# RWKV stage of a four-layer hybrid step: reversed copy of the values in two halves, later root transposes, stores issued by ScalarE

## Chip, cores and metric

One core of a Trainium2 chip runs the whole program in one launch. The metric is the device time of an execution in microseconds; lower is better. Five engines appear in the profile: TensorE (PE, with its weight loads PEld), VectorE (DVE), ScalarE (ACT), GpSimd (POOL) and SyncE (SP), which only issues transfers. 16 DMA engines carry out what is issued.

## What is computed

One step of a backbone with four layers (retention, RWKV-7, differential attention, neighbourhood attention) over 640 tokens: 128 context tokens (a prompt) and 512 latent tokens, 1024 features, all float32. The change lies in the RWKV layer, whose core in the reference is:

```python
r, k, v, g = einsum('nbld,dne->nble', stack([x_r, x_k, x_v, x_g]), w_in)
kk = k * k_k;  kk = kk * rsqrt(max(sum(kk * kk, -1), 1e-12))      # 16 heads of 64
for dr in range(2):                                               # forward, backward
    decay = exp(-exp(-softplus(-(w0[dr] + tanh(x_w @ wA[dr]) @ wB[dr])) - 0.5))
    a = sigmoid(a0[dr] + (x_a @ aA[dr]) @ aB[dr])
    kd = k * (1 + (a - 1) * k_a)
    seq = (r, decay, kd, v, kk, a)
    if dr == 1: seq = flip(seq, time)
    y_d, s_d = scan(seq, s0[dr])    # s = s*w + (s @ -kk)(kk*a)^T + v k^T ;  y = s @ r
```

Each x_n is h + xx * mu[n], a mix of a token with its neighbours. The backward direction reads the values v in reversed order of time.

## The kernel before

The layer is done in two stages. `rwkv_project` makes k, r, v and g and writes each to DRAM, and prepares every pair of heads for the scan; `rwkv_mix` loads what was written and runs the chunked scan (chunks of 64 tokens) for the eight pairs of heads.

`rwkv_project` goes through the kinds k, r, v, g in this order. For each, `mix(n)` makes eight pieces of the mixed input (VectorE makes `wm`, ScalarE casts it to a high part `wxh`, VectorE takes the low part `wxl`), and a loop over four column panels `c2` loads 256 weight columns (`weights`, L160, on SP), splits them likewise into `wh` and `wl`, and multiplies in three passes (`mm3`, L88 to L90).

- For k and r the products go feature-major into PSUM tile `pj` (three buffers), ScalarE copies them to `wst` (L1166), and SP issues the store to `dr['k']`, `dr['r']` (L1174). For k ScalarE also squares them, and TensorE sums the squares per head into `nrm` (L1173).
- After k, VectorE takes the reciprocal roots `rn` of the 16 sums (`rsqrt`, tile `wny`, L124 to L129), TensorE transposes them in five pieces (L1189), ScalarE copies them out (L1190), and SP stores them to `dr['n']` (L1191). Then come two low-rank products (`low_rank(1)` with tanh for the decay, `low_rank(4)` for a), each with its own mix, under a higher priority.
- For v the products are token-major: five tiles of 128 tokens by 256 columns per panel, copied by ScalarE to `wvs` (two buffers, L1149), stored by SP (L1150). After the four panels SP issues two copies from DRAM to DRAM that make `vr`, in which the two halves of the columns change places (L1179): one for the 128 prompt rows, one for the 512 latent rows.
- For g ScalarE takes tanh (L1163), VectorE finishes `wst` (L1164), SP stores.

`rwkv_prepare` is a generator that prepares one pair of heads at a time; two pairs are started after each panel of r. For a pair it loads k, n (as kk) and r from DRAM (L1224 to L1227) and the second low-rank factors `wBr` (L1230), which ScalarE casts (L1232); then come decay, keys and queries, whose results go back to DRAM (bk L1268, q L1271, lt and lb L1286 and L1287), and the inverse of a triangular block (L1304 to L1316).

Each engine and SP run their queue strictly in order. The order on each queue is not written by hand: a planner places every instruction by its priority (the place in the code, raised inside `high_priority`) and by a simulated time of readiness. An instruction at the head of a queue that waits holds back all behind it. All 344,356 packets of the data queues belong to one queue, SP's; before the change no other engine issues a transfer.

Of the kernel before, what the change touches and what calls it, by code (L numbers as in the profile page):

```python
# [7 lines left out]
F32 = mybir.dt.float32  # L8
# [10 lines left out]
NP = 128  # L19
# [1053 lines left out]
class Rwkv:  # L1073
    def rwkv_project(s, hT, dr):

        nc, I = s.nc, s.I
        v, act, pe, gp = nc.vector, nc.scalar, nc.tensor, nc.gpsimd
        s.pj_bufs, s.wz_bufs = 3, 2
        with s.pool(name='w1', bufs=1) as w1, s.pool(name='w1p', bufs=1, space=PSUM) as pp:
            s.pp = pp  # L1080
            T = lambda shape, name, bufs=1, dt=F32: w1.tile(shape, dt, name=name, tag=name, bufs=bufs)
            xx = T([128, 8, NT], 'wxx')

            for k, shape in (('wN', [80, 32, 32]), ('wX', [80, 32, 32]), ('wBK', [128, NCH, 128]), ('wQ', [128, 2, NCH, 64]),
                             ('wLT', [128, NCH, 64]), ('wt1', [128, NT]), ('wt2', [128, NT]), ('wt4', [128, NT])):
                T(shape, k, s.pbufs.get(k, 1))
            for a, b in PARTS:
                for g in range(0, 8, s.xx_g):
                    e = gp if s.xx_p[g // s.xx_g] == 'p' else v
                    lo, hi = max(a - 1, 1), b - 1  # L1090
                    G = slice(g, g + s.xx_g)
                    edge = lambda t, src: e.tensor_copy(xx[:, G, t:t + 1], hT[:, G, src:src + 1])
                    e.tensor_tensor(out=xx[:, G, lo:hi], in0=hT[:, G, lo - 1:hi - 1], in1=hT[:, G, lo + 1:hi + 1], op=ALU.add)
                    if a == 0:
                        edge(0, 1)
                        edge(NP - 1, NP - 2)
                        edge(NP, NP + 1)
                    else:
                        edge(NT - 1, NT - 2)
                    lo, hi = (0, hi) if a == 0 else (lo, NT)  # L1100
                    v.scalar_tensor_tensor(out=xx[:, G, lo:hi], in0=xx[:, G, lo:hi], scalar=0.5, in1=hT[:, G, lo:hi], op0=ALU.mult, op1=ALU.subtract)

            def mix(n, cuts=(0, NT)):
                parts = [(T([128, NT], 'wxh', s.x_bufs, F32R), T([128, NT], 'wxl', s.x_bufs, F32R)) for _ in range(8)]
                for a, b in zip(cuts, cuts[1:]):
                    for kc in range(8):
                        m = T([128, NT], 'wm', 2)[:, :b - a]
                        v.scalar_tensor_tensor(out=m, in0=xx[:, kc, a:b], scalar=s.vc('rwkv_mu', 8 * n + kc), in1=hT[:, kc, a:b],
                                               op0=ALU.mult, op1=ALU.add)
                        s.split(*(p[:, a:b] for p in parts[kc]), m, v)  # L1110
                return lambda kc, sl: (parts[kc][0][:, sl], parts[kc][1][:, sl])

            def low_rank(n, W, parts_, fn):
                x_ = mix(n)
                w = s.weights_list([W[0], W[1]])
                for hf in range(2):
                    ps = s.proj_T(w, 0, hf, x_)
                    t = T([128, HV], 'wlr')
                    act.activation(out=t, in_=ps, func=fn)
                    s.split(parts_[0][:, hf * HV:hf * HV + HV], parts_[1][:, hf * HV:hf * HV + HV], t)  # L1120

            W = I['rwkv_w_in'][0]
            nrm = pp.tile([128, 2, 512], F32, name='wn', tag='wn')

            for k, n in (('pj', s.pj_bufs), ('pm', 1), ('wz', s.wz_bufs)):
                for _ in range(n):
                    pp.tile([128, 512], F32, name=k, tag=k, bufs=n)
            prep = None

            def step(kind, c2):  # L1130
                for _ in range(s.preps.get(kind, (0, 0, 0, 0))[c2]):
                    with s.tc.high_priority(s.hp[4]):
                        next(prep)

            for n, base, kind in ((2, 1024, 'k'), (0, 0, 'r'), (3, 2048, 'v'), (5, 3072, 'g')):
                if kind == 'g' and s.rate:
                    s.fill_rest()
                x_ = mix(n, (0, HV, NT) if kind == 'k' else (0, NT))
                if prep is None:
                    s.tw = [T([128, NT], f'wtw{j}', 1, F32R) for j in range(2)]  # L1140
                    s.ta = [T([128, NT], f'wta{j}', 1, F32R) for j in range(2)]
                    prep = s.rwkv_prepare(w1, pp, dr)
                    next(prep)
                for c2 in range(4):
                    w = s.weights(W[:, base + c2 * 256:base + c2 * 256 + 256])
                    if kind == 'v':
                        for tt in range(5):
                            st = T([128, 256], 'wvs', 2)
                            act.copy(st, s.proj_N(w, tt, 256, x_))  # L1149
                            nc.sync.dma_start(out=dr['v'][tt * 128:tt * 128 + 128, c2 * 256:c2 * 256 + 256], in_=st)  # L1150
                        step('v', c2)
                        continue
                    sts = [T([128, NT], 'wst', 2) for _ in range(2)]
                    if kind == 'k':
                        sqs = [T([128, NT], k) for k in ('wt1', 'wt2')]
                    for hf in range(2):
                        for cc in range(2):
                            c, st = c2 * 2 + cc, sts[cc]
                            ps = s.proj_T(w, cc, hf, x_)
                            sl = slice(hf * HV, hf * HV + HV)  # L1160
                            if kind == 'g':
                                th = T([128, HV], 'wth')
                                act.activation(out=th, in_=ps, func=AF.Tanh, scale=0.5)  # L1163
                                v.scalar_tensor_tensor(out=st[:, sl], in0=th, scalar=1.0, in1=ps, op0=ALU.add, op1=ALU.mult)  # L1164
                            else:
                                act.copy(st[:, sl], ps)  # L1166
                                if kind == 'k':
                                    act.activation(out=sqs[cc][:, sl], in_=ps, func=AF.Square, scale=s.vc('rwkv_kk', c))
                    for cc in range(2):
                        if kind == 'k':  # L1170
                            c = c2 * 2 + cc
                            for tt in range(5):
                                pe.matmul(nrm[:, 0, tt * 16:tt * 16 + 16], sqs[cc][:, tt * 128:tt * 128 + 128], s.ind[:, c, :], start=c + tt == 0, stop=c + tt == 11)  # L1173
                        nc.sync.dma_start(out=dr[kind][c2 * 2 + cc], in_=sts[cc])  # L1174
                    if kind in 'rg':
                        step(kind, c2)
                if kind == 'v':
                    for a, b in ((0, NP), (NP, NT)):
                        nc.sync.dma_start(out=dr['vr'][a:b].rearrange("t (a w) -> a t w", a=2),  # L1179
                                          in_=dr['v'][a:b].rearrange("t (a w) -> a t w", a=2)[:, ::-1])  # L1180
                if kind == 'k':
                    n2, y_, t_ = (T([128, 80], k) for k in ('wn2', 'wny', 'wnt'))
                    v.tensor_scalar(out=n2, in0=nrm[:, 0, :80], scalar1=1e-12, scalar2=None, op0=ALU.max)
                    rn = s.rsqrt(w1, n2, None, None, y_, t_)
                    rt = T([128, NT], 'wst', 2)[:16]
                    for a, b in ((0, 4), (4, 5)):
                        ps = pp.tile([128, 512], F32, name='pj', tag='pj', bufs=s.pj_bufs)
                        for tt in range(a, b):
                            pe.transpose(ps[:16, (tt - a) * 128:(tt - a) * 128 + 128], rn[:, tt * 16:tt * 16 + 16], s.ident)  # L1189
                        act.copy(rt[:, a * 128:b * 128], ps[:16, :(b - a) * 128])  # L1190
                    nc.sync.dma_start(out=dr['n'], in_=rt)  # L1191
                    with s.tc.high_priority():
                        low_rank(1, I['rwkv_wA'][0], s.tw, AF.Tanh)
                        low_rank(4, I['rwkv_aA'][0], s.ta, AF.Copy)

    def rwkv_prepare(s, pool, pp, dr):
# [649 lines left out]
```

## Time and profile before

| | us |
|---|---|
| median of 3 runs | 2610.86 |
| lowest and highest | 2610.16, 2616.23 |
| profiled execution | 2608.0 |
| its span, first to last instruction | 2606.2 |

The page gives TensorE 89% of the span, VectorE 58%, ScalarE 41%, GpSimd 26%. The span in 40 slices is 65.2 us a slice; the RWKV projection lies between about 750 and 1185 us (slices 12 to 18), the scan after it up to about 1585 us. In the views by stage each engine's time is busy time in the window, followed by its count of instructions; PEclk is the share of full TensorE clock that was granted; DMA is the mean busy share of 16 DMA engines. In a timeline a row gives the start, the duration and, in brackets, how long the engine stood idle before it and for whom.

### The profile page before, as it was taken

To read this page: it belongs to the slowest core of one execution; us is meant where nothing else is said; L and a number is where in the kernel's file an instruction comes from. 1 tells how busy PE (TensorE), PEld (TensorE's weight loads), DVE (VectorE), ACT (ScalarE), POOL (GpSimd) and SP (SyncE) were. 2 spreads that over 40 slices of the span, in tenths; PEclk is the share of its full clock that TensorE was granted. 3 is DMA by queue.
4 is the path that set the end of the run, shared out by engine and by line. 5 is a ranking of instruction groups with operands and counts; after the bars stand their busy time and mean duration, and the time that the engine had idled before them with its cause. 6 is when DMAs were issued, how large, how long until landed. Compare 5 with 4: busy or idle time off the path is not lost.

```text
span 2606.2 us, 48698 instructions
## 1 busy us (share of the span) xinstructions
PE 2308.8 (89%) x18951; PEld 2086.3 (80%) x18951; DVE 1500.5 (58%) x3511; ACT 1067.3 (41%) x2405; POOL 675.5 (26%) x576
## 2 busy tenths in 40 slices
PE   7999999997988999294888997889889888999998
PEld 5888888987958889194777877688888887898888
DVE  7534343443173898394888554657776665645554
ACT  5323233332153655152333342245554433645551
POOL 3323232303210000001243433233222323332321
PEclk9999999998988889695888888899999998999999
DMA  8433333225272566367365645511111122223321
GB/s 294 131 101 102 118 101 110 90 85 188 83 262 69 166 191 216 107 193 182 102 148 136 160 126 177 175 56 48 45 55 39 51 68 56 67 76 78 77 71 57
DMA packets 344586, 303.54 MB, mean 116 GB/s; under 512 B 140220, under 2 KB 281044, under 8 KB 344356
## 3 DMA queue, kind: packets, MB, share of 16 engines
q1 hardware_dynamic: 344356, 300.44, 38.8%
q8 instruction: 149, 2.44, 0.4%
q14 instruction: 81, 0.66, 0.1%
HBM read 231.37 MB, written 64.79 MB: 114 GB/s over the span
## 4 chain that ended last, share of the span: by engine, by line
PE 34%; DVE 14%; DMA 4%; issue 3%; ACT 3%; SPq 3%; POOL 1%; ACTq 0%; DVEq 0%; POOLq 0%
PE pj L88 5%; PE pj L89 5%; PE pj L90 5%; PE oa L88 2%; PE oa L89 2%; PE oa L90 2%; DVE wtmp L1310 2%; DVE wX L1312 1%; PE nO L1024 1%; PE wsc L1439 1%; PE dtp L839 1%; PE wch L1507 1%; PE npt L1007 1%; PE wy L1541 1%; SPq L160 1%
## 5 line engine op out<-in xcount | busy, mean ns | idle before, releaser
L93 POOL TENSOR_TENSOR wl<-wr,wh 128x1024 fp32r<-128x1024 f32 (+1 forms) x168 | 371.2, 2222 | 628.5 <-ACT wh L170 490.4
L88 PE MATMUL pj<-hH,wh 128*128 128x320 f32 x1280 | 408.2, 321 | 10.5 <-ACT hH L96 7.1
L89 PE MATMUL pj<-hL,wh 128*128 128x320 f32 x1280 | 406.7, 318 | 3.0 <-POOL hL L93 2.4
L90 PE MATMUL pj<-hH,wl 128*128 128x320 f32 x1280 | 404.1, 316 | 0.1
L88 PEld LDWEIGHTS pj<-hH,wh 128*128 128x128 f32 x1280 | 246.4, 193 | 24.3 <-ACT hH L96 10.4
L89 PEld LDWEIGHTS pj<-hL,wh 128*128 128x128 f32 x1280 | 247.1, 193 | 10.6 <-POOL hL L93 3.8
L90 PEld LDWEIGHTS pj<-hH,wl 128*128 128x128 f32 x1280 | 246.5, 193 | 2.4 <-issue 1.0
L170 ACT CAST wh<-wr 128x1024 fp32r<-128x1024 f32 x168 | 175.5, 1047 | 133.7 <-PE pj L89 48.6
L88 PE MATMUL oa<-oh,wh 128*128 128x384 f32 (+1 forms) x640 | 201.6, 316 | 20.6 <-ACT wh L170 14.4
L89 PE MATMUL oa<-ol,wh 128*128 128x256 f32 (+1 forms) x640 | 199.3, 313 | 0.1
L88 PE MATMUL pj<-wh,hH 128*128 128x256 f32 x640 | 188.4, 294 | 12.2 <-DVE dr L756 7.4
L90 PE MATMUL oa<-oh,wl 128*128 128x256 f32 (+1 forms) x640 | 199.1, 312 | 0.0
L89 PE MATMUL pj<-wl,hH 128*128 128x256 f32 x640 | 186.0, 291 | 0.0
L90 PE MATMUL pj<-wh,hL 128*128 128x256 f32 x640 | 185.4, 290 | 0.0
L88 PE MATMUL pj<-wxh,wh 128*128 128x320 f32 x416 | 132.8, 327 | 53.2 <-DVE wst L1164 44.8
L88 PEld LDWEIGHTS pj<-wh,hH 128*128 128x128 f32 x640 | 127.5, 199 | 20.3 <-DVE dr L756 8.3
L88 PEld LDWEIGHTS oa<-oh,wh 128*128 128x128 f32 x640 | 122.8, 192 | 23.7 <-ACT wh L170 16.3
L89 PE MATMUL pj<-wxl,wh 128*128 128x320 f32 x416 | 134.5, 325 | 2.2 <-DVE wxl L93 2.2
L90 PE MATMUL pj<-wxh,wl 128*128 128x320 f32 x416 | 133.8, 323 | 1.9 <-DVE wl L93 1.9
L88 PEld LDWEIGHTS pj<-wxh,wh 128*128 128x128 f32 x416 | 82.1, 199 | 58.1 <-DVE wst L1164 45.1
L89 PEld LDWEIGHTS pj<-wl,hH 128*128 128x128 f32 x640 | 127.7, 200 | 0.0
L90 PEld LDWEIGHTS pj<-wh,hL 128*128 128x128 f32 x640 | 127.5, 199 | 0.0
(479 smaller groups left out, 5601.0 us busy)
## 6 DMA issues: line engine op xcount, KB each, us to landing
wr<-in_ret_w_in SPq DMA_DIRECT2D x48, 512.0 KB
wm<-in_w_mod SPq DMA_DIRECT2D x40, 512.0 KB
wr<-in_w_mod SPq DMA_DIRECT2D x32, 512.0 KB
wr<-in_rwkv_w_in SPq DMA_DIRECT2D x32, 512.0 KB
wl<-in_w_mod SPq DMA_DIRECT2D x24, 512.0 KB
wr<-in_diff_w_in SPq DMA_DIRECT2D x48, 256.0 KB
wr<-in_na_w_in SPq DMA_DIRECT2D x48, 256.0 KB
wd_bk<-wBK SPq DMA_DIRECT2D x16, 640.0 KB
```

The source lines that it names most:

```text
L88: mm(out, l[0], r[0], start=start, stop=False)
L89: mm(out, l[0], r[1], start=False, stop=False)
L90: mm(out, l[1], r[0], start=False, stop=stop)
L93: eng.tensor_tensor(out=lo, in0=src, in1=hi.bitcast(F32), op=ALU.subtract)
L160: nc.sync.dma_start(out=raw[:, :, c:c + x.shape[1]], in_=x[j * 128:(j + 4) * 128].rearrange("(k p) c -> p k c", p=128))
L170: nc.scalar.copy(hi[:, :, :n], raw[:, :, :n])
L839: pe.matmul(po, at[:, j * 128:j * 128 + 128], v_[:, vt, cc * 128:cc * 128 + 128], start=j == 0, stop=j == nt - 1)
L1007: pe.transpose(pt[:, j * 128:j * 128 + 128], P[:, j * 128:j * 128 + 128], s.ident)
L1024: pe.matmul(ot_ps[i * 64:i * 64 + 64, oc:oc + 128], vt[j][:, hc:hc + 64], pts[i][:, j * 128:j * 128 + 128], start=j == 0, stop=j == len(vt ...
L1310: v.tensor_tensor(out=t, in0=X_[:, 0:j + 1, j:j + 1].to_broadcast([80, j + 1, n]), in1=N_[:, j:j + 1, j + 1:].to_broadcast([80, j + 1, n]) ...
L1312: v.tensor_tensor(out=X_[:, 0:j + 1, j + 1:], in0=X_[:, 0:j + 1, j + 1:], in1=t, op=ALU.subtract)
L1439: pe.matmul(ps[:, u - u0, :], QT[:, u, :], TT[:, u, :], start=True, stop=True)
```

## The change

In the v loop, after panels 1 and 3, the reversed copy is issued for the 512 columns that are then complete, split in eight blocks of 64 columns instead of two of 512; the copy after the loop goes. The layout that readers of `vr` see is made by the reversed order of the blocks. The stores of k, r, v and n are issued by ScalarE; those of g stay on SP. The transposes of the roots, their copies and their store stand after the first low-rank product and inside its higher priority.

```diff
                             act.copy(st, s.proj_N(w, tt, 256, x_))
-                            nc.sync.dma_start(out=dr['v'][tt * 128:tt * 128 + 128, c2 * 256:c2 * 256 + 256], in_=st)
+                            act.dma_start(out=dr['v'][tt * 128:tt * 128 + 128, c2 * 256:c2 * 256 + 256], in_=st)
+                        if c2 % 2:
+
+                            hc = slice(c2 // 2 * 512, c2 // 2 * 512 + 512)
+                            for a, b in ((0, NP), (NP, NT)):
+                                blocks = [dr[k][a:b, hc].rearrange("t (a w) -> a t w", a=8) for k in ('vr', 'v')]
+                                nc.sync.dma_start(out=blocks[0], in_=blocks[1][:, ::-1])
                         step('v', c2)
                         continue
...
-                        nc.sync.dma_start(out=dr[kind][c2 * 2 + cc], in_=sts[cc])
+                        (nc.sync if kind == 'g' else act).dma_start(out=dr[kind][c2 * 2 + cc], in_=sts[cc])
                     if kind in 'rg':
                         step(kind, c2)
-                if kind == 'v':
-                    for a, b in ((0, NP), (NP, NT)):
-                        nc.sync.dma_start(out=dr['vr'][a:b].rearrange("t (a w) -> a t w", a=2),
-                                          in_=dr['v'][a:b].rearrange("t (a w) -> a t w", a=2)[:, ::-1])
                 if kind == 'k':
...
                     rn = s.rsqrt(w1, n2, None, None, y_, t_)
-                    rt = T([128, NT], 'wst', 2)[:16]
-                    for a, b in ((0, 4), (4, 5)):
-                        ps = pp.tile([128, 512], F32, name='pj', tag='pj', bufs=s.pj_bufs)
-                        for tt in range(a, b):
-                            pe.transpose(ps[:16, (tt - a) * 128:(tt - a) * 128 + 128], rn[:, tt * 16:tt * 16 + 16], s.ident)
-                        act.copy(rt[:, a * 128:b * 128], ps[:16, :(b - a) * 128])
-                    nc.sync.dma_start(out=dr['n'], in_=rt)
                     with s.tc.high_priority():
                         low_rank(1, I['rwkv_wA'][0], s.tw, AF.Tanh)
+                        rt = T([128, NT], 'wst', 2)[:16]
+                        for a, b in ((0, 4), (4, 5)):
+                            ps = pp.tile([128, 512], F32, name='pj', tag='pj', bufs=s.pj_bufs)
+                            for tt in range(a, b):
+                                pe.transpose(ps[:16, (tt - a) * 128:(tt - a) * 128 + 128], rn[:, tt * 16:tt * 16 + 16], s.ident)
+                            act.copy(rt[:, a * 128:b * 128], ps[:16, :(b - a) * 128])
+                        act.dma_start(out=dr['n'], in_=rt)
                         low_rank(4, I['rwkv_aA'][0], s.ta, AF.Copy)
```

## Rows read from the trace of the kernel before

**Rows 1.** The page: busy time of the engines; busy tenths in 40 slices (TensorE).
```profile
PE 2308.8 (89%) x18951; PEld 2086.3 (80%) x18951; DVE 1500.5 (58%) x3511; ACT 1067.3 (41%) x2405; POOL 675.5 (26%) x576
...
PE   7999999997988999294888997889889888999998
```
**Rows 2.** Busy time by stage; columns: window, length, five engines, PEclk, DMA share, GB/s.
```profile
824.60:836.10 11.50, 0.00 (x0) 0.00 (x0) 11.38 (x25) 3.25 (x5) 0.00 (x0) 0.51 0.30 82
...
850.00:880.00 30.00, 25.90 (x156) 23.10 (x156) 29.32 (x40) 20.33 (x40) 0.00 (x0) 0.77 0.26 87
880.00:940.00 60.00, 60.00 (x503) 58.10 (x500) 47.92 (x82) 33.92 (x80) 0.00 (x0) 1.00 0.74 230
...
960.00:1034.00 74.00, 71.51 (x665) 68.62 (x665) 65.00 (x123) 41.22 (x97) 1.12 (x2) 0.94 0.70 215
...
1061.40:1085.00 23.60, 0.00 (x0) 0.00 (x0) 0.00 (x0) 0.00 (x0) 0.00 (x0) 0.55 0.13 51
1085.00:1098.70 13.70, 0.00 (x0) 0.00 (x0) 0.00 (x0) 0.00 (x0) 0.00 (x0) 0.50 0.54 162
...
1106.20:1111.80 5.60, 5.60 (x22) 5.32 (x22) 5.56 (x16) 1.98 (x4) 3.52 (x1) 0.51 0.90 244
1111.80:1180.00 68.20, 62.07 (x531) 58.53 (x532) 62.06 (x140) 35.12 (x80) 4.18 (x8) 0.97 0.61 185
```
**Rows 3.** SP's issues in order of time: start, duration, line, tensors, count.
```profile
1033.71 0.69 SPq L1179 DMA_DIRECT2D wd_vr<-wd_v  x1
1034.50 5.69 SPq L1286 DMA_DIRECT2D wd_lt<-wLT  x2
...
1051.04 0.61 SPq L1179 DMA_DIRECT2D wd_vr<-wd_v  x1
1051.75 33.14 SPq L160 DMA_DIRECT2D wr<-in_rwkv_w_in  x1
1084.99 4.62 SPq L1271 DMA_DIRECT2D wd_q<-wQ  x1
1089.70 1.19 SPq L1230 DMA_DIRECT2D wBr<-in_rwkv_aB  x1
```
**Rows 4.** Waits, 740 to 1120 us: total us, times, longest us.
```profile
PE pj L88 <- DVE wst L1164: 44.8, 1, 44.8
PE pj L1189 <- DVE wny L129: 11.6, 1, 11.6
PE pj L88 <- ACT wvs L1149: 6.3, 1, 6.3
...
ACT wB L1232 <- DMA wBr<-in_rwkv_aB: 47.1, 5, 40.4
ACT wvs L1149 <- DMA wd_v<-wvs: 20.9, 7, 8.0
```
**Rows 5.** DMA view, 1060 to 1075 us: packets, MB, share of 16 engines.
```profile
q1 hardware_dynamic: 374, 0.77, 13.1%
```
**Rows 6.** DMA view, 1212 to 1216 us, and SP's timeline just before.
```profile
q1 hardware_dynamic: 2732, 0.66, 76.3%
...
1208.70 5.67 SPq L1415 DMA_DIRECT2D wR<-wd_q  x4
```
**Rows 7.** DMA view, 1176 to 1180 us, mostly stores of lt and lb.
```profile
q1 hardware_dynamic: 1970, 0.28, 47.0%
```
**Rows 8.** The chain that ended last: two loads of wBr, start and duration.
```profile
1014.00 2.31 DMA wBr<-in_rwkv_aB
...
1089.70 9.03 DMA wBr<-in_rwkv_aB
```
**Rows 9.** VectorE's timeline around the roots.
```profile
832.54 0.82 DVE L93 TENSOR_TENSOR wxl<-wm,wxh 128x640 fp32r<-128x640 f32 x1
...
844.06 0.89 DVE L1235 SCALAR_TENSOR_TENSOR wkk<-wkk,wkkh,wk__8958 128x640 f32<-128x640 f32 x1 [7.97 <-DMA wkk<-wd_n]
```
**Rows 10.** Line L1150: SP's issues of the v stores, ns min, median, max.
```profile
L1150 SPq DMA_DIRECT2D wd_v<-wvs x20: 319/339/1358, 967.3 to 1049.1; - x20
```

## The prediction

> **What bounds the kernel now.** I read four views in this order: busy share by slice, busy time by stage, the SP queue in order of time, and who waited for whom. TensorE is busy 89% of the span, so it is the engine to watch. But the slice row has a hole: slice 17 of 40 (1042 to 1107 us) shows a 2 where its neighbours show 9 [rows 1]. The stage table puts numbers on it: from 1061.4 to 1098.7 us, 37.3 us, TensorE, VectorE, ScalarE and GpSimd all do nothing, while the 16 DMA engines are only 0.13 busy at 51 GB/s for the first 23.6 us of it [rows 2]. A stretch in which no engine computes can only be waiting for a transfer, and whatever shortens it moves all later work forward one for one.
>
> The SP queue tells which transfer. At 1051.04 SP issues the second part of the reversed copy vr<-v (512 rows, 2048 KB, L1179). The next issue, a weight load, takes 33.14 us where a v store takes 0.34 [rows 10]; the one after it 4.62 us; only at 1089.70 comes wBr, a 64 KB load [rows 3]. ScalarE stood 40.4 us for that wBr, VectorE and TensorE stood behind ScalarE, TensorE for 44.8 us [rows 4]. So a small load that the decay step needs was queued on SP behind a big copy. Its 0.13 busy share is 2/16: the copy has two column blocks as its outer count and runs on two engines. In 15 us inside the hole 374 packets of 2 KB took 13.1% of 16 engines: 15 x 16 x 0.131 / 374 = 84 ns each [rows 5]. 1024 such rows on two engines are 512 x 84 ns = 43 us, which is the hole. The first part of the copy (128 rows, issued 1033.71) does the same on a small scale: 128 x 84 ns = 10.8 us, in which SP needs 5.69 us for two small issues, and TensorE stands 6.3 us for a ScalarE copy whose buffer waits for a v store queued there [rows 3, 4].
>
> **The change, part by part.** All against the profiled execution (2608.0 us, span 2606.2); the median of the runs shown, 2610.9, is 2.9 above it.
>
> *1. The last copy.* The new copy of 512 columns moves 64-column pieces (256 B), outer count 8. From outer count 2 on two engines I take 8 on eight engines. The second half's large part is then 512 x 8 = 4096 pieces, 512 per engine: the count per engine is as before, so all depends on what a 256 B piece costs. Nearest row: a stretch with only such loads (242 B a packet) gives 4 x 16 x 0.763 / 2732 = 17.9 ns. Stores of 128 B to DRAM, mixed with some loads, give 4 x 16 x 0.47 / 1970 = 15.3 ns. The upper bound is what SP itself needed for four loads of 640 such pieces: 5.67 us for 160 per engine, 35 ns [rows 6, 7]. So 9.2 to 18 us instead of 43. SP was held 38 us (1051.75 to 1089.7), 0.9 of the 43; now 8 to 16. wBr is issued 22 to 30 us earlier and lands in 2.3 us as at 1014 [rows 8], or again in 9.0 (1089.70 to 1098.73). Gain 22 to 37; I take 30, near the load row.
>
> In a sentence by itself: the Trainium skill (DMA: Bandwidth & Descriptors, Why a DMA increments its semaphore by 16 and not by 1) says that a transfer uses the largest number of engines up to 16 that divides the outermost counts of both sides, which would make it 8 for the new copy; the trace's 2/16 for outer count 2 agrees, and no run here yet shows the 8.
>
> *2. The small part of the last copy.* 128 pieces per engine at 17.9 to 35 ns, 2.3 to 4.5 us, instead of 10.8. The 6.3 us stand mostly goes: gain 3 to 6.3, I take 5. The v store in it also leaves SP's queue.
>
> *3. The new copies in the middle.* After panel 1 of v, SP gets 128 + 512 pieces per engine: 11.5 us (to 22) in a stretch where it used to hold nothing up. Queued behind them on SP are the weight panels of v, the bk, q and lt stores, and the k, kk, r and wBr loads, for which ScalarE and VectorE wait in order. The row nearest in length is the small part above: an 11 us hold cost TensorE 6.3 us. Loss 0 to 13; I take 5, since two v panels are by then often loaded.
>
> *4. The roots.* Today TensorE stands 11.6 us at the transposes of L1189 for the last of the reciprocal roots, which VectorE makes between the pieces of mix(1) [rows 4]. Later, TensorE does the first low-rank product there. But that product needs all eight pieces of mix(1), the last at 833.4 [rows 9] against 836.1 for the roots, and VectorE was 11.4 of 11.5 us busy in the gap [rows 2]. TensorE thus gets ahead by its first product, some 9 us. Against it: the n store comes after the product instead of before, and VectorE stood 8.0 us for kk, which is loaded from n [rows 9]; it would stand some 3 to 4 us longer, and from 850 to 880 it is the bound (29.3 of 30 us) [rows 2]. Between a gain of 12 and a loss of 4 I take a gain of 4.
>
> *5. The clock.* After the hole TensorE runs at 0.51 of its clock, the 1.2 GHz level, for the 5.6 us from 1106.2 [rows 2]; at full clock that is 2.8. Gain 0 to 4, taken as 2, as the smaller holes may still cost some.
>
> *6. Stores issued by ScalarE.* 8 + 8 + 20 + 1 = 37 issues. No row shows one on ScalarE; on SP the v stores take 0.32 to 1.36 us, median 0.34 [rows 10]. That is 12.6 us of ScalarE time, in stages where it is busy 33.9 of 60 and 41.2 of 74 us [rows 2], so most lies in its idle time; three PSUM buffers cover a 0.34 us later eviction. On the good side ScalarE stood 20.9 us for v stores to land [rows 4], 8.0 of them already in term 2; but TensorE lost only 74 - 71.5 = 2.5 us from 960 to 1034 [rows 2], so no more can come back. SP no longer waits for the k and r copies either; but the weights queued behind those stores were in time (TensorE busy 60.0 of 60 us from 880 to 940 [rows 2]), so that is worth nothing. From a gain of 2.5 to a loss of 12.6; I take a loss of 1.
>
> Sum: -30 - 5 + 5 - 4 - 2 + 1 = -35 us. 2608.0 - 35 = 2573, and some 2 more for the median: 2575 us.
>
> **Rivals.**
>
> *The pieces cost the same whatever their size* (the slower case). At 84 ns for 256 B too, each half's large part holds SP 38 us, and there are two: two holes of 45 in place of 45 + 6.3, +39, less 4 for the roots: about 2645. The hole grew from 6.3 to 45 as SP's hold went from 11 to 38 us; on that line two holds cost as much as today at 25 us each, that is from about 53 ns a piece. For it: nobody has copied DRAM to DRAM in 256 B pieces in this trace. Against it: 17.9 and 15.3 ns for loads and stores of this size [rows 6, 7]. In a sentence by itself: the Trainium skill (DMA: Bandwidth & Descriptors, Specifications) asks for at least 512 B for line rate and says that below it a read-modify-write is done, which speaks against this cut; the rows agree as far as 256 / 17.9 = 14 B/ns against 2048 / 84 = 24 go. Chance 6%.
>
> *ScalarE is held too.* If its issues wait while SP's big copy is being fed, ScalarE stands 8 to 16 us in the middle of v, with v stores of panel 2 in its queue, and TensorE behind it. Some 12 us more than term 3: 2587. For: every issue on SP was held then; against: the hold is seen on one queue alone [rows 3]. Chance 12%.
>
> *VectorE is the bound behind the hole.* It is busy 65 of 74 us before and 62 of 68 us from 1111.8 on [rows 2]; if it sets the pace, terms 2, 4 and 5 vanish (they are TensorE's), and the middle hold is its too: 30 - 8 - 1 = 21, 2590. Chance 14%.
>
> *Everything covered.* The middle copy costs nothing, the last is at its 9 us end, the roots give 8: 37 + 6 + 8 + 4 = 55, 2556. Chance 12%.
>
> *The order is not as written.* The order on every queue is worked out by a planner, so the copies and transposes can stand elsewhere than in the code; then almost any part of terms 1 and 3 may go, with the time around 2605. Chance 4%.
>
> **How the numbers follow.** The forecast, 2562 to 2588, has 52%. The range 2552 to 2600 takes in the forecast, the held ScalarE, the VectorE bound and most of the all-covered case; outside are the slower case, the order and the tails. A difference of 0.3% (7.8 us) is about what can be told from none: faster, below 2603, 0.88; same 0.05; slower 0.07.
>
> **What would show it.** Right: no stretch above 1000 us in which all engines are idle for over 15 us; during the copies DMA share near 0.5 instead of 0.13 and about 110 GB/s; the longest SP issue behind a copy 6 to 16 us; TensorE's stand at L1164 under 20 us; L1189 no longer in its waits; stores of k, r, v on a ScalarE queue at 0.3 to 0.4 us. Wrong: issues of 30 us after both large copies (the slower case), a ScalarE issue of over 5 us (held), VectorE above 95% with TensorE idle from 1000 on (VectorE bound).

## The result, and the profile after

| | us |
|---|---|
| before, in the same session | 2610.98 |
| after, median of 4 runs | 2586.49 (2578.95 to 2591.24) |
| ratio, with its 95% interval | 0.9899 (0.9868 to 0.9931) |
| profiled execution of after, its span | 2591.24, 2589.2 |
| after, measured again beside the experiments | 2581.52, ratio 0.9884 (0.9855 to 0.9913) |

By the two ratios the change gains 26 and 30 us. Line numbers of after are higher by up to 6 (v stores still L1150, copies L1156, g L1170, transposes L1193, KK load L1414).

One thing told ahead of the prediction was wrong: in the copy it is the time axis `t` that `[:, ::-1]` reverses, in both kernels. The blocks `a` only cut the columns, so any number of them gives the same `vr`; their number decides nothing but how the transfer is cut.

The page's busy tenths of TensorE: the 2 in slice 17 of [rows 1] is gone; slices 17 to 19 have 8, 6 and 5.
```profile
PE   7999999997989898865898987899899898999998
```
SP's issues of after in order of time (columns as in [rows 3]): the first half's big copy, the second half's, and what stands behind each.
```profile
998.06 0.69 SPq L1156 DMA_DIRECT2D wd_vr<-wd_v  x1
998.84 11.17 SPq L1288 DMA_DIRECT2D wd_lt<-wLT  x2
...
1011.58 0.46 SPq L1306 DMA_DIRECT2D wN<-wd_lt  x1
...
1045.92 0.67 SPq L1156 DMA_DIRECT2D wd_vr<-wd_v  x1
1047.69 8.54 SPq L1273 DMA_DIRECT2D wd_q<-wQ  x1
...
1056.85 1.02 SPq L1232 DMA_DIRECT2D wBr<-in_rwkv_aB  x1
```
The hold behind the last copy fell from 33.14 us [rows 3] to 8.54, and wBr is issued 11 us after the copy instead of 39. The waits of after, 740 to 1240 us, answer [rows 4]:
```profile
PE wtp L1424 <- DMA wKK<-wd_q: 34.1, 1, 34.1
PE wz L88 <- ACT wt L1246: 11.2, 7, 6.9
PE pj L1193 <- DVE wny L129: 4.3, 1, 4.3
...
ACT wB L1234 <- DMA wBr<-in_rwkv_aB: 8.9, 4, 4.0
ACT wE L1253 <- DMA wd_lb<-wLT: 8.4, 1, 8.4
ACT wvs L1149 <- DMA wd_v<-wvs: 6.7, 4, 4.0
```
The stand of 44.8 us is gone, ScalarE's for wBr went from 47.1 to 8.9. But TensorE's wait for KK, the first load of the scan, grew to 34.1 us. In before it was, in the same view from 1180 to 1240 us:
```profile
PE wtp L1422 <- DMA wKK<-wd_q: 18.0, 1, 18.0
```
By stage (columns as in [rows 2]):
```profile
960.00:1034.00 74.00, 65.33 (x603) 63.05 (x600) 55.08 (x101) 39.20 (x89) 1.10 (x2) 0.93 0.70 205
1043.00:1066.40 23.40, 15.27 (x117) 13.63 (x116) 20.62 (x32) 13.00 (x31) 3.30 (x3) 0.84 0.70 186
1066.40:1142.00 75.60, 68.81 (x560) 65.16 (x560) 65.89 (x149) 37.55 (x83) 5.44 (x9) 0.94 0.65 196
1142.00:1198.00 56.00, 13.04 (x280) 10.86 (x280) 25.48 (x81) 8.81 (x16) 5.61 (x5) 0.52 0.77 185
```
The last row is the new bottleneck: 56 us between the last g and the first product of the scan, with TensorE busy for 13. In before this way takes 35.9 us, with TensorE busy for 13.6. Within it all engines but SP stand still from 1169.8 to 1186.8 us, 17 us in which only transfers run; in before it is 12.

**Stretches.** Two profiles of one instruction order can stand some 8 us apart before anything that was changed (kernel before: 825.4 us at the clamp of the sums of which the roots are taken; the experiment before_eight: 833.1). So I read stretches between landmarks, from the first and last start of a line: v copies (L1149), g (L1164, now L1170), first product of the scan (L1439, now L1441), first product of the next layer (L117). Before, then after; columns: duration in ns as least, median, greatest, then first and last start:
```profile
L1149 ACT COPY wvs<-pj x20: 350/372/378, 963.6 to 1048.7; 128x256 f32<-128x256 f32 x20
L1164 DVE SCALAR_TENSOR_TENSOR wst<-wth,pj x16: 455/476/486, 1105.7 to 1180.1; 128x320 f32<-128x320 f32 x16
L1439 PE MATMUL wsc<-wTT,wQT x320: 274/275/582, 1216.0 to 1532.9; 128*128 128x128 f32 x160
```
```profile
L1149 ACT COPY wvs<-pj x20: 353/372/383, 959.3 to 1043.0; 128x256 f32<-128x256 f32 x20
L1170 DVE SCALAR_TENSOR_TENSOR wst<-wth,pj x16: 469/478/489, 1066.4 to 1142.1; 128x320 f32<-128x320 f32 x16
L1441 PE MATMUL wsc<-wTT,wQT x320: 275/275/583, 1198.4 to 1508.4; 128*128 128x128 f32 x160
```
The same landmarks, read in every profile, in us; "to scan" is the sum of the five columns before it, "all" goes from the clamp of the sums to the next layer, the last column is (1 - ratio) x 2611 from the timed runs:

| kernel | clamp to v | v | v to g | g | g to scan | to scan | all | gained |
|---|---|---|---|---|---|---|---|---|
| before | 138.2 | 85.1 | 57.0 | 74.4 | 35.9 | 390.6 | 889.6 | |
| after | 128.2 | 83.7 | 23.4 | 75.7 | 56.3 | 367.3 | 865.0 | 26 |
| after_again | 128.9 | 84.6 | 22.1 | 74.0 | 57.9 | 367.5 | 861.9 | 30 |
| before_eight | 137.9 | 78.4 | 28.1 | 73.7 | 35.9 | 354.0 | 855.6 | 31 |
| only_copy | 138.1 | 77.9 | 20.5 | 71.0 | 41.1 | 348.6 | 849.0 | 45 |
| only_stores | 134.6 | 69.5 | 62.3 | 72.0 | 51.7 | 390.1 | 889.3 | 2 |
| only_roots | 130.3 | 88.1 | 10.8 | 102.5 | 58.6 | 390.3 | 882.6 | 7 |
| copy_stores | 134.6 | 73.2 | 21.4 | 68.1 | 51.4 | 348.7 | 845.5 | 55 |
| copy_roots | 130.5 | 80.7 | 22.8 | 73.5 | 41.6 | 349.1 | 849.3 | 39 |
| inverse_first | 128.1 | 80.6 | 20.4 | 70.6 | 58.0 | 357.7 | 843.2 | 50 |
| after_redrawn | 127.9 | 85.4 | 23.9 | 74.7 | 47.7 | 359.6 | 847.0 | 40 |
| pool_copy | 127.2 | 86.9 | 12.3 | 66.5 | 65.2 | 358.1 | 847.4 | 34 |
| no_copy | 128.7 | 72.1 | 16.1 | 66.8 | 70.1 | 353.8 | 845.6 | 46 |
| after_sixteen | 128.2 | 84.0 | 21.3 | 75.8 | 57.7 | 367.0 | 860.1 | 33 |

So up to the last g the change gains 10.0 + 1.4 + 33.6 - 1.3 = 43.7 us, and 20.4 are lost again between the last g and the scan.

Two cautions. A stretch holds waiting and work, and the work differs, since the planner lays other preparation into it (689 products of TensorE in v of after, 641 in that of copy_stores). And the stages that no edit touches differ too: the scan up to the next layer takes 485 to 502 us in these profiles, the rest of the kernel 882 to 893. So "to scan" is the cleanest column for what an edit did in its own stages, and "gained" for what came of it.

### The profile page after: what moved, and what is told of

The parts are those of the page before. It is cut to its first block, busy times and chain, and to the rows that moved or that the text cites. A ratio compares the mean times of both kernels' runs of the same rounds, so it can differ in the third digit from the quotient of the medians.

```text
span 2589.2 us, 48673 instructions
## 1 busy us (share of the span) xinstructions
PE 2319.3 (90%) x18951; PEld 2090.2 (81%) x18951; DVE 1501.1 (58%) x3511; ACT 1070.2 (41%) x2405; POOL 670.7 (26%) x576
## 5 line engine op out<-in xcount | busy, mean ns | idle before, releaser
L88 PE MATMUL pj<-hH,wh 128*128 128x320 f32 x1280 | 407.9, 321 | 11.4 <-ACT hH L96 7.8
L89 PEld LDWEIGHTS pj<-hL,wh 128*128 128x128 f32 x1280 | 246.7, 193 | 11.4 <-DVE hL L93 3.8
L88 PE MATMUL pj<-wh,hH 128*128 128x256 f32 x640 | 190.0, 297 | 11.4 <-DVE dr L756 6.7
L89 PEld LDWEIGHTS oa<-ol,wh 128*128 128x128 f32 x640 | 123.1, 193 | 1.1 <-DVE ol L93 0.9
```

Source lines behind the costliest of these rows:

```text
L88: mm(out, l[0], r[0], start=start, stop=False)
L89: mm(out, l[0], r[1], start=False, stop=False)
```

## Experiments: the parts alone

`only_copy` is the kernel before with the copy in halves of eight blocks, `only_stores` with the stores on ScalarE, `only_roots` with the transposes later; `no_copy` is after with the copies taken out: the backward direction then reads v itself, and the reversal in time is left out. The edit of no_copy:

```diff
-                            for a, b in ((0, NP), (NP, NT)):
-                                blocks = [dr[k][a:b, hc].rearrange("t (a w) -> a t w", a=8) for k in ('vr', 'v')]
-                                nc.sync.dma_start(out=blocks[0], in_=blocks[1][:, ::-1])
...
-                        src = dr['vr' if d else 'v'][:, cols]...
+                        src = dr['v'][:, cols]...
```

> Only the reversed copy in halves of eight blocks; stores stay on SP, the transposes stay where they were. If the hole behind the big copy is what the change removes, this gives nearly all of it: no stretch of 37 us with all engines idle, SP's longest issue behind a copy 8 to 12 us, about 2586 to 2592 us against 2611. If the stores on ScalarE are what frees SP (rival), it gives less than half: above 2600.

Measured: 2563.24 us, ratio 0.9826 (0.981 to 0.9841). The copy alone gains 45 us, more than the whole change and some 23 more than expected; the longest group of issues behind a copy on SP took 8.00 us, and between 700 and 1300 us no stretch with all engines idle is longer than 11.3 us.

> Only the stores of k, r, v and n issued by ScalarE. If the big copy is the cause, its 33 us issue and TensorE's stand of some 45 us stay, and the time stays within 4 us of 2611. If SP's waits for the k, r and v copies were what held it, the time falls by 10 us or more.

Measured: 2607.65, ratio 0.9993 (0.9974 to 1.0011): nothing that can be told. The stage with the v panels becomes 15.6 us shorter (69.5), since the v stores no longer wait behind SP's holds, but the hole behind the copy stays, now before another instruction, and takes it back ("to scan": 390.1, before 390.6):
```profile
PE wn L1280 <- ACT wLT L1281: 45.6, 6, 33.7
```

> Only the transposes of the roots after the first low-rank product. My term was a gain of 4 us (bounds: gain of 12, loss of 4): about 2607. If VectorE is the bound there, TensorE's 11.6 us are given back before the r stage ends: 2611, or up to 4 us slower since n is stored later.

Measured: 2604.61, ratio 0.9972 (0.9954 to 0.9989). 7.9 us are gained ahead of v, but the hole is still there, inside g, and by the scan's start none of them is left (390.3); what the timed runs show, 7 us, lies in the scan:
```profile
PE pj L88 <- DVE wst L1164: 36.7, 2, 36.1
```

> The changed kernel without any reversed copy: the backward direction reads v itself, so the reversal in time of the values is left out. What the copies still cost: if the hold of SP in the middle (11 us on SP, 6.9 us of TensorE) and at the end (8.5 us on SP, 5.7 us of TensorE) reach the end of the kernel, about 13 us less than the changed kernel, 2573, and more (to 2565) if the late load for the second inverse goes too. If what follows the projection absorbs them, 2586 as the changed kernel.

Measured: 2563.65, ratio 0.9824 (0.9807 to 0.984). Compared with after, the new copies still cost 16 to 20 us in that kernel; but only_copy, which has them, is as fast. So the parts gain 45, 2 and 7 us alone and 26 to 30 together: some 25 us are lost where they meet.

## Experiments: the block count

`before_eight` is the kernel before with one number changed, and every instruction stands where it stood; `after_sixteen` likewise is after.

```diff
-                        nc.sync.dma_start(out=dr['vr'][a:b].rearrange("t (a w) -> a t w", a=2),
-                                          in_=dr['v'][a:b].rearrange("t (a w) -> a t w", a=2)[:, ::-1])
+                        nc.sync.dma_start(out=dr['vr'][a:b].rearrange("t (a w) -> a t w", a=8),
+                                          in_=dr['v'][a:b].rearrange("t (a w) -> a t w", a=8)[:, ::-1])
```

> The kernel before, with its whole copy in one piece and in its place, but eight blocks of 128 columns for two of 512; every instruction stands where it stood. It tells what the block count does alone. As the prediction has it (the copy's time goes by the number of blocks that stand outermost): SP's hold behind the big copy falls from 33.1 to 12 to 20 us, the hole on TensorE from 44.8 to 24 to 32, and the time to 2588 to 2597. If the halves alone had done it (less to copy behind the last panel): 2604 to 2612. If a piece costs the same whatever its size (four times the pieces): the hold passes 100 us, the time 2670.

Measured: 2580.74, ratio 0.988 (0.9854 to 0.9906), a gain of 31 us, 7 beyond the forecast for it. SP behind the whole copy of 2048 KB, then the waits:
```profile
1051.67 0.67 SPq L1179 DMA_DIRECT2D wd_vr<-wd_v  x1
1052.44 11.41 SPq L160 DMA_DIRECT2D wr<-in_rwkv_w_in  x1
1063.94 0.89 SPq L1271 DMA_DIRECT2D wd_q<-wQ  x1
1064.92 0.42 SPq L1230 DMA_DIRECT2D wBr<-in_rwkv_aB  x1
```
```profile
PE pj L88 <- DVE wst L1164: 15.2, 1, 15.2
```
The hold went from 33.14 to 11.41 us and the hole from 44.8 to 15.2, both below what was expected, with nothing else changed. The block count alone does what the whole change does. The halves add the 14 us between this kernel and only_copy, together with the other order that the planner made for them.

> The whole change with sixteen blocks of 32 columns in each half for eight of 64; every instruction stands where it stood. If the copies' time goes by the number of blocks up to 16: SP's holds behind the big copies fall from 11 and 8.5 to 4 to 6 us, and the time by 4 to 12 us, to 2574 to 2583. If at eight blocks the number of pieces already sets the pace (the trace shows some 1.8 ns from one 256-byte piece to the next): twice the pieces make the holds 15 to 20 us, and the time 2592 to 2605.

Measured: 2578.61, ratio 0.9875 (0.9845 to 0.9905), against 0.9884 (0.9855 to 0.9913) beside it: no difference. The holds fell by 2.5 and 0.5 us, from 10.30 and 7.52 in after_again, less than either theory had them change:
```profile
1000.72 7.85 SPq L1288 DMA_DIRECT2D wd_lt<-wLT  x2
...
1047.01 7.05 SPq L1273 DMA_DIRECT2D wd_q<-wQ  x1
```
The DMA view of 1050 to 1056 us, during a big copy, of after (eight blocks) and then of after_sixteen; packets, MB, share of 16 engines. Beside them the two blocks of before have [rows 5].
```profile
q1 hardware_dynamic: 3085, 0.79, 57.7%
```
```profile
q1 hardware_dynamic: 5838, 1.20, 135.3%
```
Two blocks are 0.131 x 16 = 2.1 engines' worth of packets, eight are 9.2, and sixteen more than all 16, so packets lie over one another in the records there. A record of a 256-byte piece is 6 x 16 x 0.577 / 3085 = 18.0 ns long, the loads' value in the prediction. The Trainium skill's rule of the outermost counts (DMA: Bandwidth & Descriptors, Why a DMA increments its semaphore by 16 and not by 1) has 2, 8 and 16 engines: the trace agrees, with 2.1, 9.2 and more than 16, as far as overlapping records can tell; that it was eight engines and not nine is not shown.

## Experiments: where the parts meet

`copy_stores` and `copy_roots` leave one part out. `inverse_first` and `after_redrawn` are after with another priority for some transfers (the copies; the loads of N), and `pool_copy` is after with the copies on GpSimd's queue; the edits of these three, in this order:

```diff
+                                with s.tc.high_priority(-3000 if c2 == 1 else 1):
-                                nc.sync.dma_start(out=blocks[0], in_=blocks[1][:, ::-1])
+                                    nc.sync.dma_start(out=blocks[0], in_=blocks[1][:, ::-1])
...
+        with s.tc.high_priority(20000):
-        nc.sync.dma_start(out=N_, in_=dr['lt'][p].rearrange("b i u s t -> (b i u) s t"))
+            nc.sync.dma_start(out=N_, in_=dr['lt'][p].rearrange("b i u s t -> (b i u) s t"))
...
-                                nc.sync.dma_start(out=blocks[0], in_=blocks[1][:, ::-1])
+                                gp.dma_start(out=blocks[0], in_=blocks[1][:, ::-1])
```

> The copy in halves and the stores on ScalarE, the roots' transposes where they were. The parts alone gave -46 (copy), -2 (stores) and -5 us (roots), the whole only -24: some 28 us go where they meet. Theory A, the second inverse: in the whole change the first half's big copy stands on SP ahead of the second inverse's load of N, so that the load waits for its hold (998.1, then 1011.6) and the inverse ends at 1111.5 instead of the 1086.4 of the copy alone. Here, in the program's order on SP, that load stands ahead of the copy: about 2561 (2555 to 2570), the second inverse stored by 1095. Theory B, SP at the hand-over: without the stores SP runs ahead and fills its queue with the scan's loads ahead of the first KK load; then the stores alone would bring the loss: about 2580 to 2590. Theory C, the roots moved behind the first low rank are what loses: 2561 too, and the next run tells it from A.

Measured: 2556.2, ratio 0.9791 (0.9771 to 0.9811): the fastest of all, 55 us ahead of the kernel before and some 25 ahead of after. It is after without the moved roots. Its middle copy holds SP as long as that of after, but what stands behind it is a weight load:
```profile
998.19 0.69 SPq L1156 DMA_DIRECT2D wd_vr<-wd_v  x1
998.92 9.96 SPq L160 DMA_DIRECT2D wr<-in_rwkv_w_in  x1
```
Its v stage takes 73.2 us, 1.1 above that of no_copy; after's takes 83.7. In after the held issue is the store of lt (998.84, above), with those of lb behind it; ScalarE, whose next result needs the buffer that an lb store reads, stood 8.4 us (the wait of wE above) and TensorE 6.9 for ScalarE. But less of the 10.5 us is waiting than it seems. The v stages by engine (columns as in [rows 2]), of after, copy_stores, no_copy and pool_copy (below):
```profile
959.30:1043.00 83.70, 75.03 (x689) 71.81 (x688) 62.88 (x116) 46.55 (x107) 1.10 (x2) 0.94 0.73 212
960.00:1033.20 73.20, 68.54 (x641) 65.75 (x641) 60.77 (x115) 42.90 (x98) 1.10 (x2) 0.97 0.76 224
958.10:1030.20 72.10, 69.49 (x677) 66.77 (x676) 57.61 (x106) 44.18 (x101) 1.10 (x2) 0.99 0.70 216
955.80:1042.70 86.90, 78.48 (x712) 76.10 (x712) 62.02 (x109) 47.43 (x108) 6.10 (x5) 0.92 0.71 208
```
TensorE stands 8.7 us in after (5.7 in after_again), 4.7 in copy_stores, 2.6 in no_copy; the rest of the difference is more work in the stage, at a lower granted clock. And pool_copy, where the copy holds no issue of SP, has 8.4. So by what is queued behind it the hold costs TensorE 1 to 4 us more, and that this is the reason is not shown; no run changed that issue alone. Theory B, that the stores bring the loss, falls; theory C, the moved roots, has this part: without them the loss is gone. By the scan's start copy_stores (348.7) is where only_copy is (348.6), so there the stores are worth nothing; the 9 us between the two in the timed runs lie, as far as the profiles show, ahead of the clamp and behind the scan's start.

> The copy in halves and the roots' transposes later, the stores on SP as before. Theory A (order of the second inverse's load and the first half's big copy): the load stands ahead of the copy here too: about 2558 (2552 to 2566). Theory B (stores off SP bring the loss): 2558 as well. Theory C (the moved roots bring it): 2580 to 2590.

Measured: 2571.11, ratio 0.985 (0.9832 to 0.9869). Between the theories: by the timed runs the moved roots cost 6 us on top of the copy, with intervals that just overlap. Up to the next layer they cost nothing (849.3 against 849.0); in the profiles the 6 us lie behind it.

> The whole change, but the first half's copies have a low priority in the planner, so that the second inverse's load of N stands two places ahead of the big copy on SP. Nothing else of the order ahead of the first KK load changes by more than a few places. Theory A: the inverse is stored some 12 to 25 us earlier than 1111.5, and the time falls to about 2565 (2558 to 2574). Theory B or C: the inverse may come earlier, but the time stays within 5 us of the whole change, 2582 to 2591.

Measured: 2560.44, ratio 0.9808 (0.9784 to 0.9832). The time is the one that theory A gave, but not by its way:
```profile
1005.68 0.40 SPq L1307 DMA_DIRECT2D wN<-wd_lt  x1
...
1007.51 0.69 SPq L1157 DMA_DIRECT2D wd_vr<-wd_v  x1
1010.63 6.31 SPq L1274 DMA_DIRECT2D wd_q<-wQ  x1
...
1110.42 0.41 SPq L1316 DMA_DIRECT2D wd_tt<-wX  x1
```
The load goes 6 us earlier, yet the inverse is stored at 1110.42, as in after (1111.48). What became shorter is v (80.6), g (70.6) and the scan (485 us for 498). A store of q is held in place of those of lt.

> The whole change with the four copies issued by GpSimd in place of SP. Theory A: SP is held by no copy, the second inverse's load goes at once, about 2563 (the time without copies), up to 2570. Theory B: the hand-over is as in the whole change, 2582 to 2591. A rival of its own: a copy in flight delays the other transfers by their shared engines whoever issued it, and then SP's loads land late by the copies' 2 x 10 us: 2575 to 2590.

Measured: 2574.97, ratio 0.9868 (0.984 to 0.9895), by the ratios 4 us ahead of after's second measurement, with intervals that overlap. SP's longest group of issues between 990 and 1045 us is 3.43 us. From the last v copy to the last g it takes 78.8 us, against 99.1 in after; v is no shorter (86.9), and g to scan grows to 65.2. So taking the holds from SP gains behind v, and some 8 us of the gain are lost at the scan's start. In the middle the copy costs as much when GpSimd issues it: ScalarE stood 10.4 us for the load of r that SP issued at 998.08, while the copy issued at 993.21 ran (4.4 us for the same load in after). So the cost does not need a hold of SP. That the engines which all transfers share are the reason, as the rival in the expectation has it, fits the DMA share of 0.99 from 996 to 1008 us, but was not shown apart: GpSimd's queue also cut the copy otherwise, 1.05 MB in 510 packets.

> The whole change, measured beside the others: every theory says 2583 to 2590, as in its first measurement (2586.5), and a second profile shows which of the stretches of the first belong to the program and which to one execution.

Measured: 2581.52, with the five stretches of the first profile to within 2 us. So the 862 to 865 us from the clamp to the next layer are the program's, and no accident of one execution.

> The whole change, with the loads of N at the highest priority: up to the second load of N the order on SP stays that of the whole change, with that load still behind the first half's big copy, but the planner lays out differently what follows. Theory A (the big copy ahead of the second inverse's load is what the whole change loses by): 2582 to 2592. Theory D (each edit makes the planner draw another order of everything behind it, and the whole change's is a poor one for no single place's sake): it may fall anywhere between 2556 and 2575, the times of the other five orders with the short copies.

Measured: 2570.72, ratio 0.9847 (0.982 to 0.9875). The load of N still stands behind the big copy and behind a hold of 11.00 us, v takes the same 85.4 us, and yet 11 to 16 us come back, behind g: 8 to 10 on the way to the scan (47.7 for 56 to 58) and 7 to 10 in the scan. Theory A falls as the whole cause; the time lies in the 2556 to 2575 of theory D.

**What is known of the loss.** From the clamp to the next layer the six kernels with the copy in halves and another order, and the one with none, take 843 to 849 us; after takes 862 to 865, and after_sixteen, which has after's order, 860. By the scan's start only_copy, copy_stores and copy_roots need 348.6 to 349.1 us, after, after_again and after_sixteen 367.0 to 367.5, and inverse_first, after_redrawn, pool_copy and no_copy lie between, at 353.8 to 359.6. So the loss, some 18 us there, is the order's that the planner made of this very combination, and it is waiting: from the clamp to the scan TensorE works 282.5 us in after and 282.7 to 284.4 in those three. Most of it lies between the last g and the scan, where TensorE stands 43.3 us in after and 26.8, 33.5 and 28.7 in the three. There SP works through its queue to the first KK load:
```profile
1144.44 0.70 SPq L1180 DMA_DIRECT2D wd_g<-wst  x1
...
1152.87 0.62 SPq L1479 DMA_DIRECT2D wUV<-wd_vr  x1
...
1175.42 0.59 SPq L1315 DMA_DIRECT2D wd_tt<-wX  x1
...
1179.96 1.44 SPq L1414 DMA_DIRECT2D wKK<-wd_q  x2
```
Between the last g store and KK stand 46 issues in after, 29.4 us of issuing in 35.5 us; in before 28, 20.1 in 22.3. 24 of the 46 are loads of values for the scan (L1479 to L1481, 16.2 us), 12 in before. In only_copy it is 37 issues in 27.9 us, in copy_stores 51 in 37.7, in inverse_first 52 in 40.7: the way goes by the number of issues, at 0.7 to 0.8 us each. What this costs by itself was not measured: inverse_first and copy_stores have more of them than after and are fast, since their last g comes earlier. How much each place has of the loss stays open. Another 8 to 10 us between after and inverse_first or copy_stores lie in the stages behind, which no edit touches. From the next layer to the end (columns as in [rows 2]), after_again and then inverse_first:
```profile
1692.60:2585.00 892.40, 817.33 (x5711) 773.68 (x5709) 541.30 (x1335) 434.24 (x1104) 259.90 (x151) 0.95 0.22 61
```
```profile
1674.60:2559.50 884.90, 810.34 (x5712) 766.88 (x5710) 542.84 (x1335) 435.03 (x1104) 260.13 (x151) 0.96 0.22 62
```
The same instructions have TensorE busy for 817 us at a granted clock of 0.95 and for 810 at 0.96. Why the clock differs stays open.

## Why the prediction was right, and where not

The forecast of 2575 lies 6.5 and 11.5 us under the two medians, both inside its likeliest band of 2562 to 2588. It is right in the main term; the sum is right partly by chance, since two errors have opposite signs: up to the last g the change gains 9 us more than the 35 of the sum, and behind it 20 are lost that no term had. Counted by parts it is the same: the copy's terms (1, 2, 3 and 5) make 32 us, and only_copy measured 45; the parts alone add up to 54, and some 25 were lost where they meet.

- **The last copy** (-30). Right. From the last v copy to the last g it is 57.0 + 74.4 = 131.4 us before and 99.1 after: -32.3, terms 1 and 5 together having been -32 (but 91.5 in only_copy, -39.9). The piece came out at 18.0 ns, the value taken, and SP's hold at 8.54 us, in 8 to 16. The halves were needed less than I thought: before_eight has 11.4 us of hold for the whole copy.
- **The small part** (-5). Right: in before_eight v becomes 85.1 - 78.4 = 6.7 us shorter, a little more than the bound of 6.3, and no other copy is in it.
- **The middle copies** (+5). Inside 0 to 13. In v TensorE stands 3 to 6 us longer in after and after_again than in no_copy, near the 5; the stage itself is 11.6 and 12.5 us longer, but 5.5 and 9.4 of that is TensorE at work. The reason given, "since two v panels are by then often loaded", covers weight loads alone: in after the held issues are stores, whose buffers ScalarE needs.
- **The roots** (-4). Between the bounds when alone (-7), but not by its way: 7.9 us are gained right where I put them and are gone by the scan's start; that 7 come out is luck. "L1189 no longer in its waits" is wrong: 4.3 of 11.6 us are left (L1193). In company the sign is wrong: +25 to +29 on top of copy and stores. No term had a moved step change the whole order.
- **The stores** (+1). In total 2 us of gain alone, within the error. The issues cost 0.33 us each as bounded:
```profile
L1150 ACTq DMA_DIRECT2D wd_v<-wvs x20: 326/326/475, 959.7 to 1043.4; - x20
```
  But that "no more can come back" was wrong of the stage: v becomes 15.6 us shorter in only_stores. I had read TensorE's idle time up to 1034 us and left out the end of v, where ScalarE's last five copies stood for stores queued on SP. The line of these copies in before, from 1020 to 1052 us (idle us and times, then the line that waited):
```profile
  DMA wd_v<-wvs: 11.4, 4
...
  PE pj L88: 6.3, 1
```
  Of the 15.6 us, 6.3 had been counted in the small part. Without a shorter hole behind it none of it reaches the end.
- **The clock** (-2). Not seen: over the whole of g the granted clock is 0.94 in both kernels, and its first 5.6 us have 0.50 in after where [rows 2] have 0.51. The hole is shorter, but TensorE still starts g at the lower level.
- **What was left out**: the way from g to the scan. I carried every microsecond of the projection on to the end, and had no term for what is late next: 20.4 us of the 43.7 were lost there. That is the largest error. The sign "no stretch above 1000 us in which all engines are idle for over 15 us" holds at the copy and fails there, with 17 us.

The rivals: pieces at the same cost whatever their size fell (four times the pieces in before_eight, a third of the hold). The Trainium skill (DMA: Bandwidth & Descriptors, Specifications), which wants 512 bytes or more, is borne out by the single record, 256 / 18.0 = 14 bytes a ns against 24 for 2 KB; the larger number of blocks outweighs it here. ScalarE was not held by SP's copy. Its timeline in after, while SP's issue of 998.84 is held to 1010, shows an issue of 0.33 us; where it stood, it waited for an lb store, not for its own issue:
```profile
1001.78 0.33 ACTq L1150 DMA_DIRECT2D wd_v<-wvs  x1
...
1012.59 0.74 ACT L1253 ACTIVATE wE<-wt 128x640 f32<-128x640 f32 x1 [8.41 <-DMA wd_lb<-wLT]
```
VectorE as the bound behind the hole fell by its sign (above 95%): 65.89 of 75.6 us busy in g, TensorE 68.81. "The order is not as written", at 4%, was put too narrowly: the copies stand where they are written, but what the planner lays around them is worth some 20 us (inverse_first against after).

## What to carry to other kernels

Look at a transfer's outermost count first: one number, two blocks to eight, gave all that the whole change of three parts did. Behind a slow issue look at what stands in the same queue and who waits for it: here TensorE stood 44.8 us because a 64 KB load was queued behind a copy. Do not carry a gain in one stage to the end without asking what is late next. Where a planner lays out the queues, time each part alone and in pairs: a part that costs nothing alone can lose 25 us in company, and here leaving it out (copy_stores) gives the fastest kernel.

## What the runs showed of the hardware

The pace of a copy from DRAM to DRAM went by its blocks more than by its pieces. Inside the copies, from the DMA view: before_eight (1054 to 1062 us), after (1050 to 1056) and after_sixteen (1002 to 1006), each in 40 equal slices of its window:
```profile
GB/s 125 141 123 115 136 172 141 151 151 166 169 174 172 177 172 177 172 177 172 177 172 177 172 177 172 177 172 177 172 177 172 177 172 177 172 177 172 177 172 177
```
```profile
GB/s 80 82 94 101 79 68 85 111 108 123 140 147 143 145 145 143 147 147 143 147 143 145 145 143 147 147 143 147 143 145 145 143 147 147 143 147 143 145 145 131
```
```profile
GB/s 339 324 274 256 222 251 243 256 219 193 213 200 205 212 215 218 206 205 211 202 209 202 183 175 169 160 166 166 165 179 177 177 172 175 177 178 175 174 175 173
```
Once only the copy runs, 8 blocks of 512-byte pieces move some 175 GB/s, 8 of 256 bytes some 145, and 16 of 128 bytes some 175, where 2 of 2 KB moved 51 [rows 2]. Per block that is 22, 18, 11 and 26 GB/s: from two blocks to eight the smaller pieces cost a block's pace far less than the number of blocks gives; from eight blocks of 512 bytes to sixteen of 128 they take back all of it. And in the stretch shown a hold of SP's queue behind its own copy did not hold ScalarE's queue, which issued in 0.33 us meanwhile.
